# A fused streaming encoder layer: other tiles for the norms, the cached keys' pieces and a branch B unit's weights

## The chip, the core and the metric

The kernel runs on one core of one Trainium2 chip. The metric is the device time of one execution in microseconds (us); runs of one kernel are compared by their median. A core has five engines that each take their instructions in order: TensorE (PE: matmuls, and PEld: its weight loads), VectorE (DVE), ScalarE (ACT), GpSimd (POOL) and SyncE (SP), which here issues nearly all DMAs, the transposing ones included. The engines wait for each other by semaphores.

## The reference

One layer over a prompt of 2048 frames and 8 running streams of 16 frames with 512 cached positions each. Cut to what matters:

```python
h = rms_norm(x, norm_g) * (1 + scale) + shift            # scale, shift, gate from c @ w_ada + b_ada
qa, ka, va, za, qb, kb, vb, zb, ga, gb = split(h @ w_in)
qa, ka = rope(qa), rope(ka)
# branch A: 4 heads, two softmaxes each, chunk-causal mask
oa = (softmax(q1 k1) - lam * softmax(q2 k2)) @ va
# branch B: 8 heads, stick-breaking
log_a = log_sigmoid(z) + reversed_cumsum(log_sigmoid(-z)) - log_sigmoid(-z)
ob = where(kpos < qpos, exp(log_a), 0) @ vb
ya = (rms_norm(oa) * silu(za)) @ w_branch_a
yb = (ob * silu(zb)) @ w_branch_b
x  = x + gate * ((sigmoid(ga) * ya + sigmoid(gb) * yb) @ w_out)
y  = rms_norm(x, final_g)                                 # and ka, va, kb, vb are outputs too
```

The running streams attend to `cache_a_k`, `cache_a_v`, `cache_b_k`, `cache_b_v` and to their own new keys and values.

## The kernel before, in words

**Numbers.** Every float32 operand of a large matmul is scaled by a power of two and split in two float16 parts, and three of the four products of parts are summed (`mm`, line 467). The scale comes from a sum of squares, so before a weight can be split its squares are summed: `sum_squares` (line 298) on ACT with an accumulator, 1024 columns at a time.

**Units and tiles.** After the modulated input is made, the work is eight units `u`, by turns branch A (even: one head with its two softmaxes) and branch B (odd: two heads). A unit has 17 steps: `NT` (16) for the streams' rows, then tiles `t` = 0 to 15 of 128 frames. A step takes on the attention scores of its tile (`scores`, matmuls at 708 and 709), and tile `t` has `t + 1` blocks of keys, so a unit's late tiles are far longer than its early ones.

- In an A unit DVE evacuates the scores (602), ACT takes exponentials with sums (134), DVE joins the two softmaxes (657), ACT and DVE split the weights in halves (318, 323).
- In a B unit ACT takes two sigmoids of each chunk (134), DVE scans (682), POOL multiplies (688), ACT casts (616) and DVE subtracts (619) for the halves.
- In both, SP then issues a transposing DMA (626, `turn`), and PE multiplies the transposed weights `wt` by the values (765 to 767 in A, 769 and 770 in B) some time later (`later_on`).

**The projection runs ahead.** The projections of all units (matmuls at 467, for B units also gate columns at 543, both reading `hs`, loaded at 444) form one line that is taken some five steps ahead of the scores (`LEAD`), by modelled time. The next unit's projection therefore begins near tile 13 of the unit before, and by then its weights must be split.

**Side work.** Three lists of small pieces are mixed in beside a step:

- `back`: the next unit's weights (`prepare_unit`): loads (350, 352), squares (298), the scale, and the cuts in halves on ACT, POOL and DVE (318, 320, 323). A B unit also has gate weights: 22 pieces against 11 for an A unit.
- `spare`: 49 pieces of norms (`one` in `norms`): each loads one block of 512 KB of the later weights or cached values (931) and squares the block loaded before.
- `cached`: 34 pieces for the cached keys (`stages`): each loads a block (939), squares the one before, and for the one before that finds the scale on PE and DVE (235, 951 to 954), splits it on POOL and DVE (320, 323) and stores it (959).

The blocks share 16 buffers of 4 KB per partition with the weights (`free`, first in, first out).

**What sets the order.** The kernel emits the pieces of a step in turn by weight (`interleaved`), and a scheduler in the build then sets each engine's order from the emitted program, on a model of the engines; instructions marked `kept` or `keep` (the squares of side work are) hold their place. In which step a piece is emitted is decided by `norm_at`, `keys_at` and `W_READY`, around lines 1043 to 1047 and 1424 to 1437.

## Time and profile before

| | us |
|---|---|
| median of 3 runs | 2222.94 |
| lowest and highest run | 2217.87, 2225.04 |
| the profiled execution | 2226.87 |
| its span, first to last instruction | 2225.0 |
| PE, DVE, ACT, POOL busy | 2048.1, 1743.2, 1605.3, 719.5 |
| mean granted clock of TensorE | 0.980 |

The units stand in the span, by the first score matmul of each, at 131.8 (unit 0, A), 294.2 (1, B), 523.7 (2, A), 698.7 (3, B), 932.2 (4, A), 1111.5 (5, B), 1349.3 (6, A) and 1529.8 (7, B). The part behind the units begins near 1760.

How to read the rows: a timeline row is start, duration, engine, line, operation, output <- inputs, shapes, and in square brackets the engine's idle time before it with what ended it. A stretch row is from:to and length, then the busy time (and instructions) of PE, PEld, DVE, ACT and POOL, the granted TensorE clock as a share of full speed, the share of the DMA engines' time, and GB/s. A row of one line's view is the operation with its count, its least, median and greatest duration in ns, and first and last start.

### The profile page before, as it was taken

How to read it: one execution, taken by the hardware profiler on the slowest of the kernel's cores; microseconds unless marked ns; L12 is line 12 of the kernel's file. 1: busy time of each engine (PE TensorE's matmuls, PEld its weight loads, DVE VectorE, ACT ScalarE, POOL GpSimd, SP SyncE). 2: the span in 40 equal slices, each digit the busy share in tenths (PEclk: the TensorE clock that was granted, in tenths of full speed). 3: DMA queues.
4: the chain of work that ended last, by engine and by line, in shares of the span. 5: the costliest groups of instructions: out<-in, count | busy, mean ns of one | idle time of the engine just before them, and what ended most of it. 6: DMA issues, size and time to landing. Idle time of an engine off the chain costs nothing.

```text
span 2225.0 us, 41210 instructions
## 1 busy us (share of the span) xinstructions
PE 2048.1 (92%) x14472; PEld 1089.3 (49%) x14472; DVE 1743.2 (78%) x3787; ACT 1605.3 (72%) x3212; POOL 719.5 (32%) x620
## 2 busy tenths in 40 slices
PE   3999999999999999999989998999997789899997
PEld 1545555555555455555554544555454344444443
DVE  5668868889886788988678888887689778787864
ACT  3978677788877787978777788876588575666531
POOL 0523024366311444742034365301345312211210
PEclk9999999999999999999999999999999899999999
DMA  9777669799796889979888999876677999889752
GB/s 333 261 246 183 128 151 224 181 221 209 184 266 164 217 199 207 212 192 227 190 207 203 182 237 223 231 171 136 151 165 174 192 280 251 217 250 235 188 155 67
DMA packets 824977, 451.03 MB, mean 203 GB/s; under 512 B 556122, under 2 KB 763274, under 8 KB 824256
## 3 DMA queue, kind: packets, MB, share of 16 engines
q1 hardware_dynamic: 823820, 448.01, 82.6%
q8 instruction: 113, 1.85, 0.4%
q14 instruction: 96, 0.79, 0.1%
q10 hardware_dynamic: 948, 0.39, 0.1%
HBM read 229.87 MB, written 86.02 MB: 142 GB/s over the span
## 4 chain that ended last, share of the span: by engine, by line
PE 27%; DVE 8%; DMA 7%; ACT 5%; issue 3%; POOL 2%; SPq 1%; DVEq 0%; POOLq 0%; ACTq 0%
PE ps_mm L467 7%; PE ps_t L543 6%; PE ps_o L1540 5%; PE ps_mm L1506 3%; DMA wt<-sc_n 2%; PE ps_s L708 1%; DVE sc_n L682 1%; PE ps_s L709 1%; DMA hs<-hT_d 1%; DMA hs<-o_d 1%; DMA dwt<-dsc 1%; ACT sc_p L134 1%; POOL sc_p L688 1%; PE ps_o L769 1%; ACT ps_s L134 1%
## 5 line engine op out<-in xcount | busy, mean ns | idle before, releaser
L688 POOL TENSOR_TENSOR sc_p<-sc_p,sc_n 128x127 f32<-128x127 f32 (+7 forms) x192 | 312.2, 1629 | 665.5 <-DVE sc_n L682 516.0
L467 PEld LDWEIGHTS <-hs 128*128 128x128 f16 x3120 | 293.3, 99 | 326.3 <-DMA hs<-hT_d 11.6
L467 PE MATMUL ps_mm<-wa,hs 128*128 128x512 f16 x1590 | 391.7, 382 | 10.8 <-DMA hs<-hT_d 9.2
L467 PE MATMUL ps_mm<-wb,hs 128*128 128x512 f16 x1530 | 380.1, 382 | 0.0
L682 DVE TENSOR_TENSOR_SCAN sc_n<-ps_s,sc_n,zero_t 128x512 f32<-128x512 f32 x192 | 245.4, 1278 | 30.6 <-ACT ps_s L134 25.1
L543 PE MATMUL ps_t<-wa,hs 128*128 128x512 f16 x1020 | 243.6, 381 | 3.3 <-DVE qst L576 2.3
L543 PEld LDWEIGHTS <-hs 128*128 128x128 f16 x1632 | 154.9, 98 | 186.2 <-DVE qst L576 6.3
L708 PE MATMUL ps_s<-k,qst 128*128 128x512 f16 (+3 forms) x640 | 222.8, 349 | 24.1 <-DVE sc_n L682 20.7
L619 DVE TENSOR_TENSOR sc_n<-sc_p,sc_n 128x128 f16<-128x128 f32 (+7 forms) x192 | 213.6, 1115 | 37.3 <-ACT sc_n L616 36.7
L134 ACT ACTIVATE sc_p<-ps_s,usc 128x512 f32<-128x512 f32 (+3 forms) x320 | 204.7, 640 | 36.0 <-PE ps_s L709 24.3
L709 PE MATMUL ps_s<-k,qst 128*128 128x512 f16 (+3 forms) x640 | 223.1, 349 | 0.0
L616 ACT CAST sc_n<-sc_p 128x128 f16<-128x128 f32 (+7 forms) x192 | 155.6, 811 | 60.6 <-POOL sc_p L688 59.9
L134 ACT ACTIVATE ps_s<-ps_s,usc 128x512 f32<-128x512 f32 (+3 forms) x320 | 197.0, 616 | 0.0
L543 PE MATMUL ps_t<-wb,hs 128*128 128x512 f16 x612 | 151.3, 382 | 7.8 <-DMA hs<-hT_d 4.4
L769 PE MATMUL ps_o<-v,wt 128*128 128x128 f16 x1088 | 134.4, 223 | 25.5 <-DMA wt<-sc_n 25.5
L1540 PE MATMUL ps_o<-wo,wb 128*128 128x512 f16 x624 | 144.8, 388 | 1.7 <-ACT wb L1314 1.7
L602 DVE TENSOR_SCALAR_CACHE_REDUCE sc_p<-ps_s,usc 128x512 f32<-128x512 f32 (+3 forms) x160 | 106.2, 664 | 33.3 <-PE ps_s L709 22.0
L1549 POOL TENSOR_TENSOR x<-m,x 128x512 f32<-128x512 f32 x32 | 47.0, 1468 | 255.4 <-DVE m L1544 161.8
L769 PEld LDWEIGHTS <-wt 128*128 128x128 f16 x1088 | 100.4, 100 | 54.3 <-DMA wt<-sc_n 29.6
L770 PE MATMUL ps_o<-v,wt 128*128 128x64 f16 x1088 | 126.2, 195 | 0.0
L682 DVE TENSOR_TENSOR_SCAN sc_n<-ps_s,zero_t 128x128 f32<-128x128 f32 (+3 forms) x128 | 104.1, 814 | 26.2 <-ACT ps_s L134 26.2
L1506 PEld LDWEIGHTS <-wa 128*128 128x128 f16 x816 | 77.8, 98 | 92.7 <-issue 6.3
(380 smaller groups left out, 4538.5 us busy)
## 6 DMA issues: line engine op xcount, KB each, us to landing
hs<-hT_d SPq DMA_DIRECT2D x132, 512.0 KB, 4.7
g_d<-gt SPq DMA_DIRECT2D x68, 256.0 KB, 4.7
out_dram<-pr SPq DMA_DIRECT2D x204, 64.0 KB, 3.3
o_d<-o SPq DMA_DIRECT2D x136, 64.0 KB, 2.3
wa<-g_d SPq DMA_DIRECT2D x17, 512.0 KB, 4.2
wb<-g_d SPq DMA_DIRECT2D x17, 512.0 KB
hs<-o_d SPq DMA_DIRECT2D x17, 512.0 KB, 4.0
wide<-in_w_ada_dram SPq DMA_DIRECT2D x8, 1024.0 KB, 12.6
```

Source lines behind the costliest of these rows:

```text
L134: i = S.activation(**kw)
L467: T.matmul(box["p"], box["h"][:, hi, k, :], U["w"][k][:, wi, :], start=(n == 0), stop=(n == 3 * KT - 1))
L543: x = T.matmul(box["g"][:, 0:gw], box["h"][:, hi, k, :], U["wg"][k // per][:, k % per, wi, :], start=(j == 0), stop=(j == 3 * KT - 1))
L616: x = S.copy(out=hi, in_=src)
L619: V.tensor_tensor(out=lo, in0=src, in1=hi, op=ALU.subtract)
L682: V.tensor_tensor_scan(out=dst[:, lo : lo + n][:, ::-1], data0=src[:, 0:n][:, ::-1], data1=zero_t[:, 0:1].to_broadcast([P, n]), initial=fi ...
L688: G.tensor_tensor(out=p[:, 0:m], in0=p[:, 0:m], in1=n[:, 1 : m + 1], op=ALU.mult)
L708: T.matmul(p[:, 0:n], qst[:, c, :], kk[:, c, 0:n], start=True, stop=False)
L709: T.matmul(p[:, 0:n], qst[:, 2 + c, :], kk[:, c, 0:n], start=False, stop=not diag)
L769: T.matmul(po[:, c * P : (c + 1) * P], wt[:, wj, :], vt[:, c, :, :], start=first, stop=False)
L1506: T.matmul(pb, st["u"][:, ui * 8 + br * 4 + k, :], wb[br * 4 + k // 2 * 2 + j][:, wi, k % 2, :], start=(n == 0), stop=(n == 11))
L1540: T.matmul(po, st["y"][:, yi * 8 + k, :], wo[j * 4 + k // 2][:, wi, k % 2, :], start=(n == 0), stop=(n == 3 * KT - 1))
```

## The change

Only the places of side work move. The pieces and their arithmetic are the same.

- Norms: before, one in each of tiles 9 to 15 of units 1 to 5, and in every tile of unit 6. Now in tiles 12 to 15 of the A units (with a weight of two), and in tiles 5 to 10 of B units 1, 3 and 5.
- Cached keys: in A units 2, 4 and 6 from tiles 9 to 12 to tiles 12 to 15. In B's tiles 0 to 7 as before.
- A B unit's weights: before, begun in the `NT` step of the A unit ahead of it and spread so as to end by tile 8. Now begun in tile 3 and ended by tile 9. Unit 0, and the B units (which prepare an A unit's weights), are as they were.

```diff
     def norm_at(u, t):
-        return u < 7 and t < NT and (t >= 16 if u == 0 else t >= 9 or u == 6)
+        if u % 2 == 0:
+            return 2 if 12 <= t < NT else 0
+        return 1 if u < 7 and 5 <= t < 11 else 0
 
     def keys_at(u, t):
-        return u in (1, 3, 5) and t < 8 or u in (2, 4, 6) and 9 <= t < 13
+        return 1 if u in (1, 3, 5) and t < 8 or u in (2, 4, 6) and 12 <= t < NT else 0
+
+    def weights_at(u):
+
+        return (1, 6) if u == 0 else (3, 10) if u % 2 == 0 else (NT, W_READY)
...
             u, t = steps[n]
             past += duration(t)
-            if t == (1 if u == 0 else NT) and u < 7:
+            start, ready = weights_at(u)
+            if t == start and u < 7:
                 back += prepare_unit(u + 1)
...
-            for fn in back[: -(-len(back) // max(1, (W_READY if u else 6) - t % NT))]:
+            for fn in back[: -(-len(back) // max(1, ready - t % NT))]:
                 side.append((1.0, back.pop(0)))
             for todo, here in ((spare, norm_at), (cached, keys_at)):
                 if todo and here(u, t):
                     left = sum(here(*step) for step in steps[n:])
-                    for _ in todo[: -(-len(todo) // left)]:
+                    for _ in todo[: -(-len(todo) * here(u, t) // left)]:
                         side.append((1.0, todo.pop(0)))
```

What the scheduler makes of it is seen in each engine's order. First ACT, where unit 1 (B) ends and unit 2 (A) begins; before, from the last cast but one of unit 1 (`CAST`, line 616) to its last (`sc_p,l<-sc_p,nm` are A's exponentials; `wacc` marks a weight's square):

```order
L616 CAST sc_n<-sc_p 128x1024
L575 COPY k<-ps_t 128x2x128
L576 COPY qst<-ps_t 128x512
L134 ACT_TABLE_LOAD
L134 ACTIVATE sc_p,l<-sc_p,nm 128x128
L134 ACTIVATE sc_n,l<-sc_n,nm 128x128
L749 ACTIVATE ob<-ps_o,usc_2856 128x128
L134 ACTIVATE sc_p,l<-sc_p,nm 128x256
L134 ACTIVATE sc_n,l<-sc_n,nm 128x256
L481 ACTIVATE pr<-ps_mm,usc_5835 128x512
L318 ACTIVATE v<-ps_mm,usc_5835 128x2x64
L616 CAST sc_n<-sc_p 128x1024
```

and now:

```order
L616 CAST sc_n<-sc_p 128x1024 x2
L575 COPY k<-ps_t 128x2x128
L576 COPY qst<-ps_t 128x512
L501 ACTIVATE qbuf_213<-rot,sq_5874 128x256
L318 ACTIVATE k_6672<-rot,sq_5874 128x2x64
L749 ACTIVATE ob<-ps_o,usc_2860 128x128
L298 ACTIVATE junk,wacc<-wb_1427 128x1024
L134 ACT_TABLE_LOAD
L134 ACTIVATE sc_p,l<-sc_p,nm 128x128
L134 ACTIVATE sc_n,l<-sc_n,nm 128x128
```

The last cast of unit 1 stood behind the table load and the exponentials of A's tiles 0 and 1; now both last casts stand ahead of them.

Second, SP at the same place: the last two large transposes of unit 1 (16 blocks each) before,

```order
L626 DMA_TRANSPOSE wt<-sc_n 128x16x128
L523 DMA out_dram<-rot 128x128
L759 DMA o_d_76<-o 128x128
L524 DMA out_dram<-pr 128x128
L527 DMA z_d_84<-pr 128x128
L523 DMA out_dram<-rot 128x128
L462 DMA rope<-in_shapes_dram 128x96
L626 DMA_TRANSPOSE wt<-sc_n 128x16x128
L626 DMA_TRANSPOSE wt<-sc_n 128x2x128
L626 DMA_TRANSPOSE wt<-sc_n 128x4x128
L444 DMA hs_182<-hT_d_59 128x2048
```

and now:

```order
L444 DMA hs_180<-hT_d_58 128x2048
L626 DMA_TRANSPOSE wt<-sc_n 128x16x128 x2
L523 DMA out_dram<-rot 128x128
L759 DMA o_d_76<-o 128x128
L524 DMA out_dram<-pr 128x128
L527 DMA z_d_84<-pr 128x128
L462 DMA rope<-in_shapes_dram 128x96 x2
L444 DMA hs_181<-hT_d_59 128x2048
L626 DMA_TRANSPOSE wt<-sc_n 128x2x128
L523 DMA out_dram<-rot 128x128
```

The two follow each other, and the stores and A's first small transposes come behind them.

Third, ACT in unit 2's tiles 11 to 13 (`wsums` and `csums` mark a norm's square, `cacc` a cached key's). Before:

```order
L298 ACTIVATE junk,wsums<-wb_1422 128x1024
L575 COPY k<-ps_t 128x2x128
L576 COPY qst<-ps_t 128x512
L318 ACTIVATE sc_n<-sc_p,r 128x1024
L318 ACTIVATE sc_n<-sc_p,r 128x384
L318 ACTIVATE k_8302<-ps_mm,usc_8227 128x2x64
L485 ACTIVATE pr<-ps_mm,usc_8227 128x256
L489 ACTIVATE szs<-ps_mm,usc_8227 128x128
L318 ACTIVATE v<-ps_mm,usc_8227 128x2x64
L298 ACTIVATE junk,cacc<-wb_1427 128x1024
L134 ACTIVATE sc_p,l<-sc_p,nm 128x1024
L134 ACTIVATE sc_n,l<-sc_n,nm 128x1024
```

and now:

```order
L298 ACTIVATE junk,wsums<-wb_1422 128x1024
L318 ACTIVATE sc_n<-sc_p,r 128x512
L318 ACTIVATE k_8278<-ps_mm,usc_8200 128x2x64
L298 ACTIVATE junk,osums<-o 128x128
L744 ACTIVATE o<-ps_o,usc_5865 128x128
L298 ACTIVATE junk,cacc<-wa_169 128x1024
L501 ACTIVATE qbuf_213<-ps_mm,usc_8200 128x256
L298 ACTIVATE junk,wsums<-wb_1425 128x1024
L134 ACTIVATE sc_p,l<-sc_p,nm 128x1024
L134 ACTIVATE sc_n,l<-sc_n,nm 128x1024
L134 ACTIVATE sc_p,l<-sc_p,nm 128x640
L134 ACTIVATE sc_n,l<-sc_n,nm 128x640
```

Two norms and a key now stand between one tile's exponentials and the next one's, where a norm and a key stood.

## The prediction

> **What bounds the kernel now.** I read the page first, then the stretches of each tile, then TensorE's timeline at its stops, then the other engines' timelines back from one stop.
>
> ```profile
> span 2225.0 us, 41210 instructions
> PE 2048.1 (92%) x14472; PEld 1089.3 (49%) x14472; DVE 1743.2 (78%) x3787; ACT 1605.3 (72%) x3212; POOL 719.5 (32%) x620
> ```
>
> TensorE (PE) is busy 92% of the span. The change alters no arithmetic, so only PE's idle time and its half-clock time can be won or lost. A mean hides where they are, so here are stretches (us of the span; then busy us of PE, PE's weight loads, DVE, ACT, POOL; granted clock, DMA share, GB/s), cut at the first score matmul of a tile.
>
> ```profile
> 347.20:389.70 42.50, 40.77 (x268) 21.10 (x267) 38.49 (x60) 31.38 (x64) 18.77 (x16) 1.00 0.91 220
> 389.70:444.20 54.50, 54.24 (x382) 28.75 (x381) 43.73 (x66) 42.62 (x87) 20.95 (x16) 1.00 0.79 180
> 482.30:523.70 41.40, 38.16 (x304) 21.08 (x304) 40.28 (x48) 40.29 (x79) 31.74 (x23) 1.00 0.98 207
> 531.60:566.90 35.30, 32.54 (x236) 17.89 (x235) 30.02 (x78) 26.63 (x60) 16.98 (x20) 0.95 0.82 227
> 628.50:658.30 29.80, 27.30 (x206) 15.54 (x204) 24.26 (x66) 21.31 (x51) 2.24 (x2) 1.00 1.07 267
> 658.30:698.70 40.40, 40.40 (x268) 21.52 (x267) 25.74 (x69) 27.75 (x53) 0.00 (x0) 1.00 0.70 160
> 890.80:932.20 41.40, 37.84 (x303) 20.98 (x303) 40.29 (x48) 40.41 (x79) 31.74 (x23) 1.00 0.99 206
> 1305.10:1349.30 44.20, 38.31 (x305) 20.94 (x305) 40.40 (x48) 40.50 (x79) 30.86 (x23) 1.00 0.99 220
> ```
>
> The first two are unit 1 (branch B), tiles 6 to 8 and 9 to 11. The third, seventh and eighth are tiles 14 and 15 of units 1, 3 and 5: DVE and ACT are both 97% busy there and PE is idle for 3.24, 3.56 and 5.89 us. The fourth is unit 2 (branch A), tiles 3 to 5, with a clock of 0.95. The fifth and sixth are unit 2, tiles 12 to 15: ACT is idle for 8.5 and 12.7 us, DVE for 5.5 and 14.7, POOL nearly always, and in the sixth PE never stops. So B's last tiles and A's first are held up by ACT and DVE, and A's last by PE.
>
> PE's timeline shows the stops at the start of units 2, 4 and 6, in A's tile 3:
>
> ```profile
> 542.92 0.23 PE L769 MATMUL ps_o<-v,wt 128*128 128x128 f16 x1 [2.76 <-DMA wt<-sc_n]
> 953.59 0.29 PE L769 MATMUL ps_o<-v,wt 128*128 128x128 f16 x1 [3.86 <-DMA wt<-sc_n]
> 1365.55 0.23 PE L769 MATMUL ps_o<-v,wt 128*128 128x128 f16 x1 [0.72 <-DMA wt<-sc_n]
> 1370.28 0.29 PE L769 MATMUL ps_o<-v,wt 128*128 128x128 f16 x1 [3.68 <-DMA wt<-sc_n]
> 543.20:546.60 3.40, 3.40 (x21) 1.72 (x18) 1.69 (x5) 1.95 (x4) 1.61 (x3) 0.51 0.66 179
> 952.90:956.20 3.30, 2.62 (x20) 1.79 (x21) 0.68 (x3) 0.62 (x2) 0.28 (x1) 0.50 0.53 103
> 1369.30:1376.00 6.70, 5.72 (x28) 2.97 (x29) 4.00 (x7) 3.24 (x6) 4.00 (x5) 0.50 0.75 187
> ```
>
> L769 is the product of B's attention weights with the values: A has begun, and B's last weights are not yet transposed. Right behind each stop the clock is granted at half. I follow the first stop back through POOL, ACT, DVE and SP (the queue that issues DMAs):
>
> ```profile
> 526.16 2.00 POOL L688 TENSOR_TENSOR sc_p<-sc_p,sc_n 128x1024 f32<-128x1024 f32 x1 [0.83 <-DVE sc_n L682]
> 530.98 1.04 ACT L616 CAST sc_n<-sc_p 128x1024 f16<-128x1024 f32 x1
> 534.54 1.22 DVE L619 TENSOR_TENSOR sc_n<-sc_p,sc_n 128x1024 f16<-128x1024 f32 x1
> 538.61 4.92 SPq L626 DMA_TRANSPOSE wt<-sc_n  x3
> 516.16 1.05 ACT L298 ACTIVATE junk<-wb 128x1024 f16<-128x1024 f32 x1
> ```
>
> POOL had finished at 528.16; ACT took up the cast 2.8 us later, DVE the rest 2.5 us after the cast's end (532.02), and SP the transpose 2.85 us after DVE's end (535.76). None of these engines stood still in between: each had other work queued ahead. The last row is part of that work: a square of a norm, in the middle of the busiest stretch.
>
> **The change, part by part.**
>
> *Squares leave B's end and A's beginning.* Their price and the waits ahead of them (the view of line 298):
>
> ```profile
> L298 ACT ACTIVATE junk<-wb x64: 1039/1057/1158, 144.5 to 1486.2; 128x1024 f16<-128x1024 f32 x64
> L298 ACT ACTIVATION_READ_ACCUMULATOR junk<-wb x64: 185/192/303, 145.4 to 1487.2; 128x1 f32 x64
>   DMA wb<-in_cache_a_k_dram: 10.3, 6
>   DMA wb<-in_cache_b_k_dram: 7.1, 2
>   DMA wa<-in_cache_b_k_dram: 3.7, 3
> ```
>
> One square costs ACT 1.057 + 0.192 = 1.25 us. The old code puts a norm in each of B's tiles 9 to 15 and begins the next B unit's weights in A's first step. Norms and weights together are about four squares in B's tiles 14 and 15, 5 us of ACT. The quoted orders show what this does to the chain: the last two casts now stand ahead of the table load and the exponentials, and on SP the two big transposes stand together, where five stores and a load stood between them. So the delays of 2.8 and 2.85 us have lost their cause; together they are more than any of the three stops (2.76, 3.86, 3.68). I take the stops as gone: 2.76 + 3.86 + 0.72 + 3.68 = 11.0 us. If the cast alone gets earlier and SP stays as late, it is about 2.8 per boundary, 8.4 us.
>
> *The half clock goes with the stops.* 3.4 × 0.49 + 3.3 × 0.50 + 6.7 × 0.50 = 6.7 us. Bounds: 0 if the stops only move, 6.7 if they vanish. [...]
>
> *The stretch of B's tiles 14 and 15 itself.* ACT gets 5 us back, but DVE's 40.28 of 41.40 us are untouched, since a square of 1024 columns has no DVE part. So no more than DVE's own idle time can go: 1.12, 1.11 and 3.80 us, 6.0 in all. I take 2: PE's stops need not end with DVE's.
>
> *Norms and keys enter A's tiles 12 to 15.* By the rules of the diff there are 8 + 4 = 12 squares in those four tiles, where 4 + 1 = 5 were: 7 × 1.25 = 8.8 us more of ACT against 21.1 us idle. A key also puts a subtraction of 1.28 us and four short operations of 0.15 on DVE:
>
> ```profile
> 633.13 1.28 DVE L323 SCALAR_TENSOR_TENSOR wb<-wb,csc,wb 128x1024 f16<-128x1024 f32 x1 [0.65 <-POOL wb L320]
> 632.20 1.06 ACT L298 ACTIVATE junk<-wb 128x1024 f16<-128x1024 f32 x1 [2.88 <-DMA wb<-in_cache_a_k_dram]
> 639.47 0.23 PE L765 MATMUL ps_o<-v,wt 128*128 128x128 f16 x1 [2.50 <-DMA wt<-sc_n]
> 1040.26 0.23 PE L765 MATMUL ps_o<-v,wt 128*128 128x128 f16 x1 [3.22 <-DMA wt<-sc_n]
> 1457.56 0.23 PE L765 MATMUL ps_o<-v,wt 128*128 128x128 f16 x1 [2.79 <-DMA wt<-sc_n]
> 1041.60:1045.00 3.40, 3.40 (x20) 2.25 (x19) 2.85 (x10) 0.35 (x1) 1.12 (x1) 0.50 0.94 253
> 1458.10:1461.40 3.30, 3.30 (x23) 2.29 (x21) 0.52 (x1) 0.00 (x0) 0.00 (x0) 0.50 0.75 200
> ```
>
> Three more keys are 3 × 1.88 = 5.6 us of DVE against 20.2 idle, and POOL is free. PE's work is the cover; what can break it is a square that waits for its load at the head of ACT's queue, with the exponentials, A's products on PE, and SP's transposes behind it. The second row is such a wait; 11 key squares waited 10.3 + 7.1 + 3.7 = 21.1 us in all, and few of those reached PE. Lower bound: the present waits of A's tiles 9 to 11 go, some 4 us gained. Upper bound: each of the 12 keys in A holds PE for the mean wait of 1.9 us, 23 us. In the new order loads stand a tile or more ahead of their squares, and these tiles are longer, so I stay nearer the low end: 4 us lost. The three PE stops quoted are at A's tiles 11 and 12; the last had no key's wait ahead of it, so I count nothing for them, and for the low end 8.5 us plus the half clocks behind the second and third (the last two rows), 3.4 us.
>
> *Norms enter B's tiles 5 to 10.* One square of 1.25 us a tile; ACT is idle for 11.1 us in tiles 6 to 8 and 11.9 in 9 to 11, and PE is the bound in the second. I take 1 us lost; without that cover it is 18 × 1.25 = 22.5 us, which the idle rows exclude, so 6 as the upper bound.
>
> *A B unit's weights, in A's tiles 3 to 9.* Same instructions and DMAs, later by a tile or two.
>
> ```profile
> 545.78 4.18 DVE L323 SCALAR_TENSOR_TENSOR wa<-wb,sw,wa 128x512 f16<-128x512 f32 x4 [0.31 <-ACT wa L318]
> 549.88 4.14 DVE L323 SCALAR_TENSOR_TENSOR wa<-wa,sw,wa 128x512 f16<-128x512 f32 x4
> 1543.37 9.06 SPq L626 DMA_TRANSPOSE wt<-sc_n  x4
> 1561.30 2.32 PE L467 MATMUL ps_mm<-wa,hs 128*128 128x512 f16 x5 [5.89 <-DMA hs<-hT_d]
> ```
>
> The cuts hold DVE for 8.3 us in one run, yet in 531.6 to 566.9 PE was idle for 35.30 − 32.54 = 2.76 us, which is the stop ahead of them: projections covered the run. I take nothing, and 2 us per unit, 6, as the upper bound. They end by tile 9, and the next unit's projection begins near tile 12. The last two rows are at unit 7, where a load of `hs` stands behind four transposes of 9.06 us. The new order puts a fifth, of six blocks beside the 40 of the four, ahead of it; by 9.06 us for 40 blocks, 1.4 us. I take 1 lost.
>
> **Sum:** −11.0 − 6.7 − 2 + 4 + 1 + 0 + 1 = −13.7 us. The profiled execution took 2226.87 us (its span and 1.9 around it), 0.18% over the median of the runs; it would take 2213. From the median, 2222.94 − 13.7 = 2209 us.
>
> **The rivals.**
>
> *The DVE keeps the bound (no change).* For it: DVE is as full as ACT at B's end, and all it can give back there is 6.0 us. Then casts wait less on ACT, but the subtractions behind them still come late, and the stops at A's tile 3 only shrink. 6.0 won and 4 + 1 + 1 lost: 2223. Against it: in the new DVE order the last subtractions stand ahead of the evacuations of A's tiles 2 and 3.
>
> *ACT stops at squares in A's last tiles (slower).* For it: the 21.1 us of such waits, and a DMA share of 1.07 in 628.5 to 658.3, where more loads now come. It concerns 16 tiles (four each in units 0, 2, 4, 6). If half open a PE stop like the three quoted, 2.8 us on average and 1.7 of half clock, that is 8 × 4.5 = 36 us against the 17.7 of the stops won: 2222.94 + 18 = 2241. It decides from four such tiles. Against it: ACT and DVE idle there, and PE's stretch without a stop.
>
> *More is won.* The stops at A's tiles 11 and 12 go too (8.5 and 3.4) and all 6.0 of B's end: 17.7 + 11.9 + 6.0 − 6 = 29.6, 2193.
>
> *The change does not do what it says*: the orders quoted exclude it.
>
> **How the numbers follow.** My forecast 0.58, more won 0.06, no change 0.20, slower 0.16. A measurement of this kernel tells 0.3%, 6.7 us, from no change, so faster is under 2216.3 and slower over 2229.6. The forecast's own spread (its clock term can halve, its cost terms double) leaves a little of it within 0.3%; the rest follows the cases: faster 0.61, same 0.22, slower 0.17. The range reaches from near the case of more won to just past no change and leaves out the slower case's centre: 2194 to 2231. The forecast's own range is 2199 to 2218.
>
> **What would show it.** Right: in tile 3 of units 2, 4 and 6 no PE wait at L769 over 1 us and a clock near 1.00; ACT well under 97% in B's tiles 14 and 15, with DVE still at 97%; in A's tiles 12 to 15 ACT some 9 us busier per unit and PE still without idle time. Wrong: ACT waits at L298 for loads in A's last tiles with PE stops behind them at L765 (the slower rival), or stops of the old size at L769 behind a DVE that never rests (no change).

## The result: 0.5% slower, and the profile after

| | us |
|---|---|
| kernel before, median of 5 runs | 2223.15 (2217.87 to 2227.34) |
| changed kernel, median of 5 runs | 2233.55 (2229.38 to 2237.23) |
| ratio, with its 95% interval | 1.0049 [1.0033, 1.0066] |
| forecast | 2209 (2194 to 2231) |

The prediction said faster; the changed kernel is slower, by some ten us. The page of the changed kernel begins with these lines (its execution took 2235.06 us):

```profile
span 2233.3 us, 41216 instructions
PE 2055.2 (92%) x14472; PEld 1090.5 (49%) x14472; DVE 1745.3 (78%) x3787; ACT 1603.0 (72%) x3212; POOL 708.1 (32%) x620
```

The engines have as many instructions as before, and PE, DVE and ACT are busy for nearly as long; the stretches tell where the time went. The columns are those of the prediction's stretches (us; busy us of PE, its weight loads, DVE, ACT, POOL; clock, DMA share, GB/s). First A's tiles 2 and 3 of units 2, 4 and 6, then B's tiles 14 and 15 of units 1, 3 and 5, then A's tiles 12 to 15 of unit 2:

```profile
537.60:547.00 9.40, 9.31 (x81) 5.25 (x81) 8.59 (x31) 8.91 (x25) 2.96 (x5) 1.00 0.87 167
955.20:964.50 9.30, 9.27 (x80) 5.19 (x79) 8.49 (x31) 8.85 (x25) 2.93 (x5) 1.00 0.92 159
1371.40:1380.70 9.30, 9.27 (x80) 5.19 (x79) 8.50 (x31) 8.84 (x25) 2.93 (x5) 1.00 1.00 157
486.30:529.40 43.10, 37.18 (x259) 20.24 (x259) 40.06 (x45) 35.56 (x68) 28.16 (x21) 0.88 0.80 172
906.80:947.00 40.20, 34.76 (x259) 18.80 (x259) 39.48 (x45) 35.31 (x68) 27.18 (x20) 0.96 0.90 180
1323.00:1363.20 40.20, 34.77 (x259) 18.84 (x259) 39.47 (x45) 35.28 (x68) 27.19 (x20) 0.96 0.85 182
629.60:711.70 82.10, 78.96 (x542) 42.97 (x541) 57.36 (x153) 52.91 (x113) 5.59 (x6) 1.00 0.88 221
```

I call "lost" what PE cannot win back in a stretch: its idle time, plus the stretch's length times what the clock lacks to 1. In A's tiles 2 and 3 the loss is 0.1 us, where it was 17.9 us in the three units. In B's tiles 14 and 15 it is 5.9 + 5.2, 5.4 + 1.6 and 5.4 + 1.6, together 25 us, where it was 12.7. ACT is relieved there (83 to 88% busy instead of 97%), DVE is still full (98% in the last two). The whole account, in us lost, before and after:

| place | before | after | difference | predicted |
|---|---|---|---|---|
| A, tiles 2 and 3, units 2, 4, 6 | 17.9 | 0.1 | -17.8 | -17.7 |
| B, tiles 14 and 15, units 1, 3, 5 | 12.7 | 25.4 | +12.7 | -2 |
| B, tiles 0 to 11, units 1, 3, 5 | 19.5 | 26.5 | +7.0 | +1 |
| A, tiles 0, 1 and 4 to 11, units 2, 4, 6 | 10.3 | 15.8 | +5.5 | 0 |
| A, tiles 12 to 15, units 2, 4, 6 | 5.8 | 6.0 | +0.2 | +4 |
| unit 7 | 47.3 | 47.2 | -0.1 | +1 |

The differences add up to 7.5 us; the spans differ by 8.3. Each kernel was profiled in one execution, and the five executions of the kernel before spread over 9.5 us, so rows of one or two us are not to be read closely. What the change was forecast to win at A's start it won to the tenth. It was spent at the end of B, some twenty us earlier. PE's timeline there (start, duration, instruction, in brackets the wait ahead of it):

```profile
513.61 0.38 PE L708 MATMUL ps_s<-k,qst 128*128 128x512 f16 x1 [1.39 <-DVE sc_n L682]
515.00 0.38 PE L708 MATMUL ps_s<-k,qst 128*128 128x512 f16 x1 [0.62 <-DVE sc_n L682]
519.35 0.59 PE L708 MATMUL ps_s<-k,qst 128*128 128x512 f16 x1 [2.97 <-DVE sc_n L682]
938.01 0.58 PE L708 MATMUL ps_s<-k,qst 128*128 128x512 f16 x1 [2.96 <-DVE sc_n L682]
1354.17 0.41 PE L708 MATMUL ps_s<-k,qst 128*128 128x512 f16 x1 [2.97 <-DVE sc_n L682]
```

and the stretch behind the third of them:

```profile
518.10:524.90 6.80, 5.55 (x21) 2.53 (x21) 6.80 (x8) 2.75 (x6) 2.00 (x1) 0.50 0.64 147
```

The last score matmuls of tile 15 wait for DVE's scan (L682), which reads `ps_s`, the tile that they write: up to 2.97 us, and the clock is at half from 518.1 to 524.9. Before the change the longest such wait here was one of 1.7 us, in the timeline of the kernel before:

```profile
518.64 0.38 PE L708 MATMUL ps_s<-k,qst 128*128 128x512 f16 x1 [1.70 <-DVE sc_n L682]
```

What the build did with PE's order in tile 15 of unit 1 explains why it cannot do anything else meanwhile (S: a score chunk, P: projection matmuls, V: products with the values, T: transposes; with their counts):

```
before   S T6 V19 P1 S P19 V12 S V4 S V12 P11 S P13 V1 S V4 S V1 T6 V14 S V10 P18 V8
changed  S V9 S V17 P15 S P3 T6 P2 V4 S V4 S V17 S V3 P9 T6 P9 S P6 V2 S V7
```

Between the third chunk and the sixth stood 24 projection matmuls and 17 products; now it is 5 and 25, and the waits are ahead of the fourth, fifth and sixth. The tile as a whole has 44 projection matmuls instead of 62 and 63 products instead of 85: the others stand outside the tile now. The timelines of DVE and POOL show what the longest wait is made of:

```profile
515.05 3.05 DVE L619 TENSOR_TENSOR sc_n<-sc_p,sc_n 128x1024 f16<-128x1024 f32 x1
518.03 1.27 DVE L682 TENSOR_TENSOR_SCAN sc_n<-ps_s,sc_n,zero_t 128x512 f32<-128x512 f32 x1
515.03 2.00 POOL L688 TENSOR_TENSOR sc_p<-sc_p,sc_n 128x1023 f32<-128x1023 f32 x1 [1.47 <-DVE sc_n L682]
```

The scan stands behind a subtraction (L619) of 3.05 us. The prediction's own row had 1.22 us for it. This one began 0.02 us after a product on POOL (L688) that took 2.00 us; the one behind the other would be 3.22, an estimate near its 3.05.

This is most of the loss. The time of L619 alone in tiles 14 and 15 of units 1, 3 and 5 (length, then DVE busy with L619 and its count, clock, DMA share, GB/s), first before the change, then after it:

```profile
482.30:523.70 41.40, 10.90 (x8) 1.00 0.98 207
890.80:932.20 41.40, 10.90 (x8) 1.00 0.99 206
1305.10:1349.30 44.20, 10.92 (x8) 1.00 0.99 220
```

```profile
486.30:529.40 43.10, 14.93 (x8) 0.88 0.80 172
906.80:947.00 40.20, 14.52 (x8) 0.96 0.90 180
1323.00:1363.20 40.20, 14.50 (x8) 0.96 0.85 182
```

The same eight subtractions take 3.6 to 4.0 us longer in each unit, 11.2 us in all, where DVE has no time to spare; the row lost 12.7.

### The profile page after: what moved, and what is told of

The parts are those of the page before. It is cut to its first block, busy times and chain, and to the rows that moved or that the text cites. A ratio compares the mean times of both kernels' runs of the same rounds, so it can differ in the third digit from the quotient of the medians.

```text
span 2233.3 us, 41216 instructions
## 1 busy us (share of the span) xinstructions
PE 2055.2 (92%) x14472; PEld 1090.5 (49%) x14472; DVE 1745.3 (78%) x3787; ACT 1603.0 (72%) x3212; POOL 708.1 (32%) x620
## 3 DMA queue, kind: packets, MB, share of 16 engines
q8 instruction: 113, 1.85, 0.4%
## 5 line engine op out<-in xcount | busy, mean ns | idle before, releaser
L688 POOL TENSOR_TENSOR sc_p<-sc_p,sc_n 128x127 f32<-128x127 f32 (+7 forms) x192 | 312.6, 1632 | 560.6 <-DVE sc_n L682 503.4
L467 PEld LDWEIGHTS <-hs 128*128 128x128 f16 x3120 | 293.0, 99 | 323.5 <-issue 18.5
L467 PE MATMUL ps_mm<-wa,hs 128*128 128x512 f16 x1794 | 443.0, 381 | 4.7 <-DVE v L323 4.6
L467 PE MATMUL ps_mm<-wb,hs 128*128 128x512 f16 x1326 | 342.8, 384 | 7.8 <-DMA hs<-hT_d 5.4
L682 DVE TENSOR_TENSOR_SCAN sc_n<-ps_s,sc_n,zero_t 128x512 f32<-128x512 f32 x192 | 245.3, 1278 | 43.0 <-ACT ps_s L134 38.0
L708 PE MATMUL ps_s<-k,qst 128*128 128x512 f16 (+3 forms) x640 | 222.8, 349 | 43.8 <-DVE sc_n L682 36.7
L619 DVE TENSOR_TENSOR sc_n<-sc_p,sc_n 128x128 f16<-128x128 f32 (+7 forms) x192 | 229.6, 1199 | 32.5 <-ACT sc_n L616 32.2
L543 PE MATMUL ps_t<-wa,hs 128*128 128x512 f16 x1020 | 249.8, 384 | 5.3 <-DMA hs<-hT_d 2.7
L1547 PE MATMUL ps_o<-wo,wa 128*128 128x512 f16 x624 | 141.4, 381 | 1.7 <-ACT wa L1320 1.7
L769 PE MATMUL ps_o<-v,wt 128*128 128x128 f16 x1088 | 130.4, 222 | 12.1 <-DMA wt<-sc_n 12.1
L508 POOL TENSOR_TENSOR rot<-pr,rope 128x256 f32<-128x256 f32 x68 | 63.0, 927 | 219.2 <-ACT pr L481 153.2
L602 DVE TENSOR_SCALAR_CACHE_REDUCE sc_n<-ps_s,usc 128x512 f32<-128x512 f32 (+3 forms) x160 | 106.1, 664 | 20.1 <-PE ps_s L709 13.3
L134 ACT ACTIVATE sc_p<-sc_p,nm 128x1024 f32<-128x1024 f32 (+4 forms) x96 | 85.8, 894 | 48.6 <-DVE nm L636 48.6
```

The source lines that it names most:

```text
L134: i = S.activation(**kw)
L467: T.matmul(box["p"], box["h"][:, hi, k, :], U["w"][k][:, wi, :], start=(n == 0), stop=(n == 3 * KT - 1))
L543: x = T.matmul(box["g"][:, 0:gw], box["h"][:, hi, k, :], U["wg"][k // per][:, k % per, wi, :], start=(j == 0), stop=(j == 3 * KT - 1))
L602: V.tensor_scalar(out=dst[:, lo : lo + n], in0=p[:, 0:n], scalar1=sc_pos, scalar2=None, op0=ALU.mult, op1=ALU.max, accum_out=job["mx"][:, ...
L619: V.tensor_tensor(out=lo, in0=src, in1=hi, op=ALU.subtract)
L682: V.tensor_tensor_scan(out=dst[:, lo : lo + n][:, ::-1], data0=src[:, 0:n][:, ::-1], data1=zero_t[:, 0:1].to_broadcast([P, n]), initial=fi ...
```

## Experiments

All times are medians; the ratio is to runs of the kernel before on the same chip. "Norms", "keys" and "weights" are the three edits of the change: `norm_at`, `keys_at` and `weights_at`.

### The edits apart

**Weights alone** (to the kernel before; `weights_at` is called as in the change):

```diff
+    def weights_at(u):
+        return (1, 6) if u == 0 else (3, 10) if u % 2 == 0 else (NT, W_READY)
```

> Only the B unit's weights move (A's tiles 3 to 9); norms and keys stand as before. Theory N (the norms leaving B's last tiles bring the new waits of score matmuls L708 on DVE's scans, 36.7 us in all in the changed kernel against 20.7): no such wait here, L708 on scans near 20 us, and the stops at L769 in A's tile 3 (2.76, 3.86, 3.68) shrink, so 5 to 12 us faster than before, 2211 to 2218. Rival W (the run of cuts, now in tiles 4 and 5, delays the evacuation of the projections): three waits of 1.5 us of L467 on DVE near A's tile 6 and further ones, no gain left, 2223 to 2235. Rival R (any new order of the scheduler is some us off, whatever moves): no particular place, within 8 us of 2223 either way.

Measured: 2251.20 us, 1.0133 [1.0111, 1.0155].

**Norms alone** (the changed kernel, with the keys and weights put back):

```diff
-        return 1 if u in (1, 3, 5) and t < 8 or u in (2, 4, 6) and 12 <= t < NT else 0
+        return 1 if u in (1, 3, 5) and t < 8 or u in (2, 4, 6) and 9 <= t < 13 else 0
-        return (1, 6) if u == 0 else (3, 10) if u % 2 == 0 else (NT, W_READY)
+        return (1, 6) if u == 0 else (NT, W_READY)
```

> Only the norms move (A's tiles 12 to 15, B's tiles 5 to 10). Theory N: the whole of the loss and more, since the weights' gain is missing: a wait of near 3.0 us of L708 on a scan in tile 15 of units 1, 3 and 5, L708 on scans 35 to 45 us in all, 2233 to 2242. Rival W: no loss, 2217 to 2226. Rival R: no particular place, within 8 us of 2223.

Measured: 2247.09 us, 1.0115 [1.0092, 1.0138].

**Keys and weights** (the changed kernel, with the norms put back):

```diff
-        if u % 2 == 0:
-            return 2 if 12 <= t < NT else 0
-        return 1 if u < 7 and 5 <= t < 11 else 0
+        return (1 if t >= 9 or u == 6 else 0) if 0 < u < 7 and t < NT else 0
```

> Keys and weights move, the norms stand as before. Theory N: as the weights alone, within 4 us of it, and 5 to 14 us faster than before. Rival W: 2223 to 2235. Rival R: within 8 us of 2223, and not tied to the run of the weights alone.

Measured: 2235.64 us, 1.0056 [1.0040, 1.0072].

**Norms and keys** (the changed kernel, with the weights put back: the second line pair of "norms alone" only).

> Norms and keys move, the weights stand as before. Theory N: slower than before by 10 to 19 us and slower than the whole change by up to 9, with the three waits of near 3.0 us of L708 in tile 15 of units 1, 3 and 5. Rival W: within 4 us of 2223. Rival R: within 8 us of 2223.

Measured: 2242.60 us, 1.0089 [1.0068, 1.0110].

Three of the four are slower than the whole change, and the fourth, keys and weights, can't be told from it. So no edit has a price of its own: weights cost 29 us beside the old norms and keys, and win 9 beside the new ones. In the trace of weights alone A's tiles 2 and 3 win 12 us (17.9 lost before, 6.2 now), but A's tiles 4 to 11 lose 16 more and unit 7 loses 15 more.

What does go with one edit is B's end: in every kernel with the norms moved (norms alone, norms and keys, the change) there are the stops ahead of three of the last chunks, the longest 2.5 to 3.0 us; in the two kernels with the old norms the end of unit 1 is that of the kernel before, one wait of 1.7 us. PE's order in tile 15 is the same, instruction for instruction, in the kernels with the norms moved (the change, these two, and "no norm in B" below), and there the eight subtractions take 14 to 16 us; the order of the kernel before is that of the other two here and of the runs below that have real squares in B's tiles 13 to 15 and a whole product, and there they take 10.7 to 10.9.

The run of norms alone also shows a second price, in PE's and DVE's timelines in A's tile 4 of unit 2 (the profiled execution was its fastest, 2234.97 us, 12 below the median, so the trace shows less than the whole loss):

```profile
554.28 2.17 PE L467 MATMUL ps_mm<-wa,hs 128*128 128x512 f16 x7 [4.24 <-DVE v L323]
549.17 4.80 DVE L323 SCALAR_TENSOR_TENSOR wa<-wb,sw,wa 128x512 f16<-128x512 f32 x5
```

Five cuts of the gate weights hold DVE for 4.80 us, the halves of `v` stand behind them, and the next projection behind those: 4.24 us, in all three units. The prediction had seen the run of cuts and said that projections covered it. With the weights moved too, this stop is 1.5 us, in tile 6.

### Norms back at B's end, and where else they stand

**Three norms back at B's end** (the changed kernel):

```diff
-        return 1 if u < 7 and 5 <= t < 11 else 0
+        return 1 if u < 7 and t in (5, 6, 7, 13, 14, 15) else 0
```

> The whole change, but three of the six norms of a B unit stand in tiles 13 to 15 again, as before the change, in place of tiles 8 to 10. Two theories. (1) The loss sits at B's end: with no square in B's last tiles PE's order there has no projections left between the last score matmuls, and each of them waits for the scan (2.97 us at L708). With the squares back these three rows of 2.97 us and the half clock behind them go, and with them the 12.7 us that tiles 14 and 15 of units 1, 3 and 5 had lost; A's tile 3 stays without its stops: 2233.6 - 12.7 = about 2221. (2) The lateness is conserved: DVE is full at B's end, and what does not show there as a wait for the scan shows behind it as a wait for a transposed weight. Then the stops at L769 of 2 to 4 us come back in A's tiles 2 to 4 of units 2, 4 and 6, with their half clock, and the time stays within 0.3% of the change, 2227 to 2240.

Measured: 2217.42 us, 0.9974 [0.9961, 0.9987]. PE's order in tile 15 is again the old one, and so is the wait, in PE's timeline in unit 1:

```profile
523.10 0.38 PE L708 MATMUL ps_s<-k,qst 128*128 128x512 f16 x1 [1.69 <-DVE sc_n L682]
```

The stretches of tiles 14 and 15 of units 1, 3 and 5, and of A's tiles 2 to 4 of unit 2:

```profile
485.80:528.20 42.40, 39.51 (x305) 22.15 (x305) 39.79 (x48) 40.38 (x78) 31.50 (x24) 0.96 1.01 211
900.95:942.40 41.45, 38.21 (x305) 21.12 (x305) 40.42 (x48) 40.14 (x78) 32.26 (x24) 1.00 0.96 206
1312.00:1354.30 42.30, 39.43 (x305) 22.15 (x305) 39.70 (x48) 40.34 (x78) 31.55 (x24) 0.96 0.97 206
532.40:551.10 18.70, 18.07 (x157) 10.56 (x156) 15.86 (x57) 17.42 (x46) 7.49 (x9) 1.00 0.81 175
```

The three B ends lose 12 us instead of 25, as the first theory had it, and 305 matmuls are in the stretch again instead of 259. The lateness was not conserved: A's first tiles stay without a stop over 1 us. One line of the change is worth 16 us, more than the whole change. Not all of it is B's end, which is 13 us: the same line also takes the norms out of B's tiles 8 to 10, unit 7 wins 10 us, and B's tiles 0 to 11 and A's 4 to 11 lose 9.

**No norm in B** (the changed kernel):

```diff
-            return 2 if 12 <= t < NT else 0
-        return 1 if u < 7 and 5 <= t < 11 else 0
+            return 2 if 12 <= t < NT else 1 if 8 <= t < 12 else 0
+        return 0
```

> The whole change, but no norm in a B unit: those of B's tiles 5 to 10 go to A's tiles 8 to 11, one each. If the squares in B's middle are what loses time there (7 us more idle and half clock in B's tiles 0 to 11 than before the change, by the traces), this time comes back: 2233.6 - 7 = about 2227, and the waits of 1.5 to 2.2 us at L708, L235 and L543 in B's tiles 4 to 10 look as before the change. If any other order of the same work is some us off, wherever the squares stand, it is 2231 or more, with new stops in A's tiles 8 to 11.

Measured: 2269.19 us, 1.0194 [1.0174, 1.0213]. The stops in B's middle stay without the norms (6.2 us idle in tiles 6 to 8 of unit 3, 4.2 in the changed kernel), B's ends lose 34 us, and unit 7 loses 11 us more. So taking all squares out of B does not bring back the 7 us of B's tiles 0 to 11. The traces of all runs split that row. In units 3 and 5 it goes with the keys: the five kernels with the keys in their old places lose 15 to 18 us there, the thirteen with the keys moved 19 to 32, keys alone 23 against 16 before. In unit 1, ahead of which no key has moved, it goes with norms in B's tiles 5 to 7: 4 to 8 us are lost with them and 2 to 4 without, but 9 in this run, for which no cause is shown.

**Norms of before, one tile early** (the kernel before):

```diff
-        return u < 7 and t < NT and (t >= 16 if u == 0 else t >= 9 or u == 6)
+        return u < 7 and t < NT and (t >= 16 if u == 0 else t >= 8 or u == 6)
```

> The kernel before, with the norms of units 1 to 5 beginning at tile 8 in place of 9; weights and keys untouched. By the terms of the prediction this is worth nothing: 2223, within 0.3%. If every other order of these pieces costs some 10 us because all the work around was fitted to this one, 2230 or more, with stops at places that have no norm in them.

Measured: 2234.11 us, 1.0038 [1.0025, 1.0052]. An edit that my terms price at nothing costs almost as much as the whole change. Its new stops are in A's tiles 11 to 14, where in units 2 and 4 norms stand in both kernels: 1.4 to 3.4 us at L765 and L708. A's tiles 9 to 13 lose 24 us instead of 15.

**Short squares at B's end** (the changed kernel):

```diff
+                if u in (1, 3, 5) and t >= 13: side.append((1.0, lambda: sum_squares(ident, 8, tiny.tile([P, 1], F32, tag="jk", name="jk"), keep=True)))
                 qk = scores(units[u], t, made)
```

> The whole change, with an extra square of 8 columns in each of B's tiles 13 to 15, held in its place on ACT like a norm's square, with no load and next to no time. If a norm's square at B's end helps as a fixed point in ACT's order, this gives most of what the three real squares gave: 2217 to 2222, one wait of 1.7 us at L708. If it helps by the time that the build's model gives it on ACT, because the score matmuls are then placed later on PE, among projections, this changes nothing: three waits at L708 at the end of units 1, 3 and 5, the longest about 3.0 us, and 2233 within 0.3%.

Measured: 2229.09 us, 1.0030 [1.0015, 1.0045]. A fixed point in ACT's order does not bring the time that real squares bring (2217). The time is the one that the second theory gave, its stops are not. B's ends lose 12 us, as with the real squares, and the 3.0 us are gone; PE's order in tile 15 is neither the old one nor that of the change. In their place, in all three units, PE stops in A's tile 1, and A's tiles 0 and 1 lose 12 us instead of 3. In this run's timelines:

```profile
530.35 0.30 PE L561 MATMUL ps_t<-id,k 128*128 128x128 f16 x2 [2.55 <-DVE k L323]
528.21 2.08 DVE L323 SCALAR_TENSOR_TENSOR k<-rot,sq,k 128x128 f16<-128x128 f32 x1
528.09 2.06 POOL L688 TENSOR_TENSOR sc_p<-sc_p,sc_n 128x1024 f32<-128x1024 f32 x1
```

A cut of 128 columns, 0.34 us in the median, lasts 2.08 beside the same product of POOL, and PE's next transpose stands behind it.

**Norms in B only at its end** (the run with three norms back, again changed):

```diff
-            return 2 if 12 <= t < NT else 0
-        return 1 if u < 7 and t in (5, 6, 7, 13, 14, 15) else 0
+            return 2 if 12 <= t < NT else 1 if 9 <= t < 12 else 0
+        return 1 if u < 7 and 13 <= t < NT else 0
```

> As the run with three norms back at B's end, but B's tiles 5 to 7 have none; A's tiles 9 to 11 take one each. If squares in B's tiles 5 to 7 cost the 3 to 4 us per unit that B's tiles 2 to 8 show over the kernel before, it is 2217.4 - 8 = about 2209. If A's tiles 9 to 11 are the worse place (the run without any norm in B lost there and in A's last tiles), stops at L765 grow in A's tiles 9 to 13: 2222 or more.

Measured: 2225.62 us, 1.0015 [1.0003, 1.0027]; the profiled execution was its fastest (2219). By the time A's tiles 9 to 11 are the worse place, by 8 us. The second theory's sign did not come: in the trace A's tiles 9 to 13 lose 10 us instead of 17 and B's tiles 0 to 11 win 8, while A's tiles 12 to 15 lose 7 more. Where the slower executions lose more is not shown.

### The product on POOL in halves

To the changed kernel, to the run with three norms back, and to the fastest version (below):

```diff
-        G.tensor_tensor(out=p[:, 0:m], in0=p[:, 0:m], in1=n[:, 1 : m + 1], op=ALU.mult)
+        for i in range(0, m, 512): G.tensor_tensor(out=p[:, i : min(i + 512, m)], in0=p[:, i : min(i + 512, m)], in1=n[:, i + 1 : min(i + 512, m) + 1], op=ALU.mult)
```

> The whole change, with POOL's product of 1024 columns (L688) issued as two instructions of 512. Theory of the shared port: a subtraction on DVE (L619), 1.2 us alone, lasts up to 3.05 us when it begins beside POOL's product of 2.0 us, because it waits for the whole instruction; with halves of about 1.0 us no L619 lasts over 2.3 us, its mean falls from 1.20 us to under 1.10, and the waits of 2.97 us at L708 at the end of B fall to under 2.2: about 5 us won, 2228. Rival: the order alone makes these stops, and DVE's length does not matter; the waits at L708 stay, and the time is 2233 or, with POOL's fixed cost per instruction, more.

> As the run with three norms back at B's end, with POOL's product (L688) in two instructions of 512 columns. Theory of the shared port: no L619 over 2.3 us (up to 3.02 now), DVE saves some 15 us in all, of which the part at B's ends and in unit 7 counts: 2217.4 - 5 = about 2212. Rival: what it saves is lost again where the build now orders things otherwise (half the product on the changed kernel won 12 us at B's end and lost 13 at A's start): 2217 to 2230.

> As the fastest version so far (three norms at B's end, old place of the weights, keys and norms in A's last tiles: 2203.0 us), with POOL's product (L688) in two instructions of 512 columns. Theory of the shared port: the saving of 4.5 us that the halves brought with the later weights (2217.4 to 2213.0) does not hang on the weights: about 2198, no L619 over 2.3 us. Rival: the saving was that order's luck: 2200 to 2212.

Measured: 2231.64 us, 1.0035 [1.0020, 1.0049]; 2212.95 us, 0.9957 [0.9942, 0.9971]; 2206.47 us, 0.9925 [0.9913, 0.9938]. Against the same kernels with whole products that is 2 and 4 us won and 3 lost, each within what the intervals leave open. What was claimed of the instruction's length held (that a port is shared is my assumption, and no run shows it): in the first pair the mean of L619 falls from 1.20 to 1.08 us, and no wait at L708 in B's tiles 14 and 15 is over 0.7 us. The view of L619 has minimum, median and maximum in ns; first of the changed kernel, then of the same with halves:

```profile
L619 DVE TENSOR_TENSOR sc_n<-sc_p,sc_n x192: 263/1212/3051, 298.5 to 1766.7; 128x1024 f16<-128x1024 f32 x80, 128x128 f16<-128x128 f32 x16, 128x256 f16<-128x256 f32 x16, 128x384 f16<-128x384 f32 x16
```

```profile
L619 DVE TENSOR_TENSOR sc_n<-sc_p,sc_n x192: 261/1200/2149, 298.4 to 1759.7; 128x1024 f16<-128x1024 f32 x80, 128x128 f16<-128x128 f32 x16, 128x256 f16<-128x256 f32 x16, 128x384 f16<-128x384 f32 x16
```

No subtraction lasts longer than 2.15 us, and B's ends lose 13 us instead of 25. But the new order has other stops in A's tiles 0 to 5, up to 2.0 us and with half clock: 17 us lost there against 4.3. So it is shown that the longest subtraction gets shorter with POOL's product, 2.15 us instead of 3.05, and that halving the product is a gain of its own is not: the third kernel had no use for it. Nor can the 12 us at B's ends be put down to the shorter subtractions alone (9.7 to 10.6 us for the eight), since PE's order in tile 15 changed with them. Long subtractions alone do not cost them either: with three norms back and halves the eight take 13.1 to 13.4 us, in an order of PE of its own, and B's ends lose 12 us as without halves.

### What the fast version needs

**Old weights, three norms back at B's end** (the changed kernel with the norms as in the run with three norms back and the weights put back; keys as changed):

```diff
-        return 1 if u < 7 and 5 <= t < 11 else 0
+        return 1 if u < 7 and t in (5, 6, 7, 13, 14, 15) else 0
-        return (1, 6) if u == 0 else (3, 10) if u % 2 == 0 else (NT, W_READY)
+        return (1, 6) if u == 0 else (NT, W_READY)
```

> As the run with three norms back at B's end (2217.4 us), but a B unit's weights are prepared from A's first step on again, as before the change. That run had no stop of over 1 us in A's tiles 2 to 5 of units 2, 4 and 6, although the squares of the norms stood at B's end. Theory: the weights' squares, loads and cuts at A's start are what made the casts late; with them back the stops at L769 in A's tile 3 (2.8 to 3.9 us each) and their half clock come back, 17.7 us in all: about 2235. Rival: the placing of the keys and norms took the stops away; then no stop over 1 us at L769, and 2217 to 2224.

Measured: 2203.02 us, 0.9912 [0.9895, 0.9930], faster than both kernels. Both theories missed: neither do the stops come back in full, nor is the weights' move worth nothing. It costs 14 us here. The page's first lines, and PE's timeline at A's tile 3 of units 2, 4 and 6:

```profile
span 2201.2 us, 41247 instructions
PE 2041.6 (93%) x14472; PEld 1089.2 (49%) x14472; DVE 1747.5 (79%) x3787; ACT 1603.7 (73%) x3212; POOL 717.7 (33%) x620
```

```profile
545.21 0.23 PE L769 MATMUL ps_o<-v,wt 128*128 128x128 f16 x1 [1.63 <-DMA wt<-sc_n]
954.52 0.23 PE L769 MATMUL ps_o<-v,wt 128*128 128x128 f16 x1 [1.86 <-DMA wt<-sc_n]
1363.84 0.23 PE L769 MATMUL ps_o<-v,wt 128*128 128x128 f16 x1 [2.41 <-DMA wt<-sc_n]
```

Unit 2, tiles 5 to 13, here and, below it, in the run with the weights moved:

```profile
560.90:655.30 94.40, 93.35 (x675) 52.50 (x673) 83.68 (x236) 76.60 (x180) 22.70 (x24) 1.00 0.74 187
```

```profile
551.10:658.30 107.20, 102.20 (x717) 56.05 (x716) 91.50 (x253) 85.78 (x198) 31.89 (x33) 0.98 0.80 194
```

The stops at A's tile 3 are smaller than before the change (1.6 to 2.4 us instead of 2.8 to 3.9), and no half clock follows them. From tile 5 to 13 PE is idle for 1.05 us of 94.40; with the weights in tiles 3 to 9 for 5.0, at a clock of 0.98. Over the three A units, tiles 6 to 13, that is some 3 us lost against 23, while A's tiles 2 to 5 lose 6.5 against 1.5.

**Keys alone** (to the kernel before, in effect):

```diff
-        return u in (1, 3, 5) and t < 8 or u in (2, 4, 6) and 9 <= t < 13
+        return u in (1, 3, 5) and t < 8 or u in (2, 4, 6) and 12 <= t < NT
```

> The kernel before, with the cached keys' pieces alone moved from A's tiles 9 to 12 to its tiles 12 to 15. If the keys' move wins A's tiles 9 to 13 (the stops at L765 of 2.5 to 3.2 us there and their half clock, 15 us before the change, 1.9 in the fastest version), this is about 2223 - 13 = 2210. If it wins only with the norms that make room, 2220 or more. Since keys and weights together gave 2235.6, a result near 2210 would put the cost of the weights' later start at some 25 us beside the old norms.

Measured: 2224.13 us, 0.9998 [0.9985, 1.0011].

**The same norms, with the old keys and weights** (the fast version with the keys put back to `9 <= t < 13`):

> The kernel before, with the norms alone moved: three in B's tiles 5 to 7, three in 13 to 15, two in each of A's last four tiles; keys and weights at their old places. If the norms that leave A's and B's middle bring the win, about 2205 to 2212. If the keys do, about 2220 or more, with stops at L765 at A's tiles 11 to 13 as before.

Measured: 2232.49 us, 1.0032 [1.0017, 1.0047].

Nothing for the keys and 9 us lost for the norms, but 20 us won for both. The traces say where: in A's tiles 9 to 13 of units 2, 4 and 6 the kernel before loses 15 us, keys alone 15, these norms alone 10, both 2. Of these four only the one with neither kind of square in A's tiles 9 to 11 is rid of the stops at L765. That alone is not enough: norms and keys moved, without the three norms at B's end, lose 9 us there. With the old keys 17 us are also lost in A's tiles 14 and 15 (4 in the fast version), where PE waits for loads of `hs` at L467, 2.5 and 2.0 us; why these come late there is not shown.

**Weights from tile 1** (to the fast version):

```diff
-        return (1, 6) if u == 0 else (NT, W_READY)
+        return (1, 6) if u == 0 else (1, 9) if u % 2 == 0 else (NT, W_READY)
```

> As the fastest version (weights from A's first step, done by tile 6: 2203.0 us), with a B unit's weights begun in tile 1 and done by tile 9; begun in tile 3 and done by 10 it was 2217.4. If the weights' later start costs by itself because their loads and cuts meet the longer tiles, this lies between, about 2208 to 2214, with stops at L765 and L467 in A's tiles 6 to 12 between those of the two. If each order is a matter of its own, it may be anywhere, 2200 to 2225, and the stops stand at other places.

Measured: 2223.53 us, 1.0002 [0.9991, 1.0013]. Not between the two: since a unit's first step is `NT`, a start in tile 1 is two steps later and costs 20 us, one in tile 3 is four steps later and costs 14. Both later starts cost; the cost does not grow with the lateness.

## Why the prediction was wrong, step by step

- **The stops at L769 and their half clock, -17.7:** came as forecast, -17.8. The reason given for it, norms' squares at B's end together with weights at A's start, is borne out in part. With no norm at B's end A's tiles 2 and 3 lose nothing (0.0 to 0.2 us), whether the weights are moved or not. With the old norms, moving the weights alone leaves 6.2 us of 17.9. With three norms back in tiles 13 to 15 the loss is nothing with the weights moved to tile 3, 5 to 6 us with the old weights, and 10 with the weights from tile 1. So both count. But the same three squares and the same weights stand in the kernel before, which loses 17.9: what the other norms in B's tiles 9 to 12 and in A do to it stays open.
- **"The stretch of B's tiles 14 and 15 itself", -2: the step that failed.** It measured +12.7. The step took PE's order in this stretch as given, subtracted ACT's squares, held DVE's 40.28 us for untouched because a square has no DVE part, and bounded the rest by DVE's idle time. But the build sets the order from its model, and the eight subtractions of this stretch took 14.5 to 14.9 us instead of 10.9 in the new order. With the squares gone it places the third to the sixth score chunk of tile 15 with few projections between them, and PE then waits for a DVE that has no time to give. I had compared the orders of ACT and SP behind this place and not PE's order in it. Putting three squares back restored the old order, the 10.9 us and the old loss: 13 us undone. A short square in the same place undoes as much here by another order and loses it again in A's tile 1. What of a real square restores the old order, its time in the model or its load, stays open. The row also read DVE and ACT as 97% busy in all three units; in unit 5 they were 91 and 92% busy (40.40 and 40.50 of 44.20 us).
- **DVE's durations:** the 1.22 us of L619 are from a row in which POOL stood still. In the stretch in question L619 runs beside POOL's product and lasts up to 3.05 us. The kernel before already had one of 2.38 us, so its traces could have warned.
- **"Norms enter B's tiles 5 to 10", +1 and at most 6:** B's tiles 0 to 11 lost 7.0 more, above the bound. Some 4 us of it are in unit 1, where they go with the norms, though the run without any norm in B did not win them back. The rest is in units 3 and 5 and goes with the keys, for which the prediction had no term in B.
- **"The cuts hold DVE ... projections covered the run", 0:** wrong. Beside the moved norms the run stops PE for 4.2 us in each of three units, and the weights' later start costs 14 us in the otherwise best version.
- **Norms and keys in A's last tiles, +4:** +0.2 in the change. What leaves A's tiles 9 to 11 for them is the part that pays: with the old weights and three norms at B's end, A's tiles 9 to 13 win 13 us. The lower bound had 8.5 and 3.4 us for those very stops, and I had counted nothing.
- **The rivals:** that DVE keeps the bound was right about B's end as far as ACT's relief is worth nothing there, but it allowed for no loss. ACT's stops at squares in A's last tiles, my slower rival, did not come: the stretch of unit 2 is idle for 3.1 us of 82.1.
- **What was to show it:** no wait over 1 us in A's tile 3, clock 1.00, ACT well under 97% and DVE full at B's end: these came as written, in a slower kernel. ACT in A's tiles 12 to 15 was only 4 to 5 us busier per unit, not 9, and PE there was idle for 1.0 to 3.1 us. A list that looks only where a gain is expected can't tell a gain from a transfer; the waits at L708 were not on it.

## What to carry to other kernels

Where a scheduler sets the order, taking work away from one engine is not a subtraction: compare the new order of the bounding engine, and of those that wait for it, in the very stretch that was relieved, before pricing anything there. Here a shift by one tile that should have been neutral cost 0.4%, and the weights' edit cost 29 or 14 us or won 9 and the keys' won nothing or 29 by what stood beside them, so price pairs of edits, not edits, and try each with the others undone: the best version here dropped one edit and half of another. Durations for a sum are to be read beside the neighbours that the instruction will have, DVE's with two inputs from SBUF beside POOL above all (L619: 1.22 us alone, up to 3.05 beside L688).

## What the runs showed of the hardware

In these traces a DVE instruction that reads two tensors from SBUF can last longer beside POOL's product. In the changed kernel L619 of 1024 columns takes 1.20 to 1.23 us where POOL is idle (28 of them) and 1.20 to 3.05 beside L688 (2.00 us), the cut of 128 columns 0.34 in the median and up to 2.08, and with POOL's product in halves the longest L619 is 2.15. The longest began 0.02 us after POOL's product; that it stood still until the product's end is my estimate, from 2.00 and 1.22 us added up. The scans of 512 columns (L682, `sc_n<-ps_s,sc_n,zero_t`), whose scores come from PSUM, take 1.27 to 1.28 us beside L688 (49 of them) and where POOL is idle. The cut of `k` shows it in one line of the kernel: with its input in SBUF (`rot`) or in PSUM (`ps_mm`), in the changed kernel (least, median and greatest ns),

```profile
L323 DVE SCALAR_TENSOR_TENSOR k<-rot,sq,k x68: 325/344/2084, 77.0 to 1467.9; 128x128 f16<-128x128 f32 x68
L323 DVE SCALAR_TENSOR_TENSOR k<-ps_mm,usc,k x68: 322/342/352, 225.4 to 1695.5; 128x128 f16<-128x128 f32 x68
```

Beside L688 the cuts from `rot` take 2.08 us (three of them) and those from `ps_mm` 0.32 to 0.35 (29).

The half clock also followed a stop shorter than the 2.76 us of the prediction, one of 2.55 us (short squares; the clock was at half from 530.5 to 533.9, and a matmul of L769 took 0.29 us there), while stops of 1.63, 1.86 and 2.41 us in the fast version were not followed by one (0.22 us a matmul behind the last two, a clock of 1.00 around the first). The stop at the same place in unit 6 of the short squares was followed by none. The rows of the short squares, first around the stop that is followed by half clock, then around the one that isn't:

```profile
527.10:530.50 3.40, 0.64 (x8) 0.47 (x8) 3.40 (x5) 1.44 (x3) 3.40 (x4) 1.00 0.69 156
530.50:533.90 3.40, 3.40 (x34) 2.80 (x33) 3.21 (x10) 2.77 (x4) 0.37 (x1) 0.50 0.32 74
1363.30:1366.70 3.40, 1.71 (x19) 1.11 (x16) 3.30 (x5) 1.73 (x3) 3.40 (x6) 1.00 0.99 207
1366.70:1370.10 3.40, 1.55 (x28) 1.40 (x29) 3.40 (x5) 1.58 (x3) 1.80 (x2) 1.00 0.23 55
```

In the traces of the kernel before and of the changed kernel the stretches of half clock (15 and 17) begin whole multiples of 3.413 us apart, and all but the one that ends each profile last one to four times that; one is from 543.24 to 546.65 before the change. Cut into windows of that length, units 0 to 6 of the two traces have 809 windows at full clock. The nine with PE idle the longest, 2.03 to 3.11 us, are all followed by a window at half clock. Of the other 800 two are, with 1.98 and 1.64 us, while ten with 1.65 to 1.85 are not. What goes with the half clock in these traces is PE's idle time, as the profile has it, in such a window, more than the length of one stop: 2.76 us in the first row above, 1.69 and 1.85 where the second stop fell across two windows.
